# Expert stages that gather and scatter by exact 0/1 matrices over split tokens and rows

## The chip, the core and the metric

The kernel runs on one core of a Trainium2 chip, in one launch. TensorE (PE) multiplies, VectorE (DVE), ScalarE (ACT) and GpSimd (POOL) work beside it, and SyncE (SP) issues nearly all loads of weights from the chip's memory. The metric is the device time of the launch in microseconds (us).

## The reference, cut to what matters

Two transformer blocks of two layers each run over 256 tokens of 1024 features, all in float32. The change is in the second block, whose layers end in a mixture of experts: each token picks two of 32 experts, and each expert is a gated product of width 512.

```python
experts = grp[:, None] * EXPERTS_PER_GROUP + top_local        # two per token
gates = p_grp * jax.nn.softmax(top_logit, axis=-1)
...
def expert_block(args):
    xb, e = args
    return (jax.nn.silu(xb @ w_gate[e]) * (xb @ w_up[e])) @ w_down[e]
...
y_assign = y_slots[dest] * g_sorted[:, None].astype(h.dtype)
y = jax.ops.segment_sum(y_assign, tok_sorted, num_segments=t)
...
x = x + hybrid_mixer(rmsnorm(x, norm_mix[l]), ...)
x = x + hierarchical_moe(rmsnorm(x, norm_ffn[l]), ...)
```

All 32 experts' three matrices are read in each layer: 32 x 6 MiB.

## The kernel before

The tokens lie in two tiles of 128 (t = 0, 1). Each expert has 64 slots; a token sits in the slot that its place among the expert's tokens gives (`pos`, from 1 on; 0 for a token that is not the expert's). Four experts' slots, 256, are one group, and two experts are a pair `pr`.

For a group, `normed` builds `one`, a matrix from tokens to slots: the row of a token holds, in its slot, the token's norm factor `rt.r`. It is made by `hots`, one DVE step for each expert and token tile (L1667). `weighted` builds `wt` in the same way with the expert's gate as the factor. `gather` multiplies the token tiles, as they stand in `h` (float32, the features of a chunk eight apart), by `one` (L1684): 8 chunks of features by 2 token tiles, 256 columns each. ACT and DVE copy the sums, times the norm's gain, into `xg` (L1697, L1695). It also transposes `wt` on PE (L1701), and ACT copies the result to `back` (L1703).

For each expert `gate_up` multiplies its 64 slots by the gate and up weights (L1714), and ACT and DVE form silu(gate) x up (L1718, L1719). `turn` transposes that (L1725, L1727). For each pair `down` multiplies by the down weights (L1737), and ACT and DVE copy the two sums to `ys` (L1742, L1743). `scatter` multiplies `ys` by `back` into `total` (L1749), four banks that hold the sums for all tokens until the layer's end. A pair's scatter stands on PE behind the next pair's first `gate_up`.

PE gives a float32 product two passes in the trace (two rows each). Products of tiles of type fp32r take one pass; elsewhere in the kernel, as in `mm3` (L332 to L334), operands are split into an fp32r high part and an fp32r rest, and three such products stand for one exact product.

The order of each engine's work is the order in which the code issues it. Weights come through a ring of tiles of 1 MiB in the order of use: `Ring.pump` issues a load on SP's queue (L143) as soon as a tile of the ring is free, and a tile becomes free when its last product is done. The ring has 5 tiles for the whole kernel, 8 for the second block, 2 from each layer's output projection on, and `RING3` more in the expert stage. SP's queue works in order. At pair 1 stands `leftover`: SP and the other engines read the largest number of tokens of an expert and branch (L1613, L1614); the branch is not taken here. Loads that are issued behind it in the code wait for it.

## Time and profile before

| | us |
|---|---|
| median of 3 runs | 2049.39 |
| lowest and highest run | 2048.31, 2050.05 |
| span of the profiled execution | 2045.9 |
| PE busy | 1912.5 (93%) |
| PE's weight loads busy | 1452.7 (71%) |
| DVE busy | 800.5 (39%) |
| ACT busy | 653.5 (32%) |

Only the span of the profiled execution is known; the runs' times, which include what lies around a span, are 2.4 to 4.2 us above it. A busy engine is not a bound by itself: PE's passes overlap, and the stages differ in what they wait for. So the page is read by stretches: which engine has no gaps there, and what the others, and the queue of loads, wait for. A window's row gives the stretch and its length in us, then the busy us (and the number of instructions) of PE, PE's weight loads, DVE, ACT and POOL, and last the clock that TensorE was granted (1.00 is 2.4 GHz, 0.50 is 1.2 GHz), the DMA engines' share and GB/s; a window asked for SP has only the last three. Row after row of a timeline or chain begins with start and length in us.

### The profile page before, as it was taken

To read this page: it belongs to the slowest core of one execution; us is meant where nothing else is said; L and a number is where in the kernel's file an instruction comes from. 1 tells how busy PE (TensorE), PEld (TensorE's weight loads), DVE (VectorE), ACT (ScalarE), POOL (GpSimd) and SP (SyncE) were. 2 spreads that over 40 slices of the span, in tenths; PEclk is the share of its full clock that TensorE was granted. 3 is DMA by queue.
4 is the path that set the end of the run, shared out by engine and by line. 5 is a ranking of instruction groups with operands and counts; after the bars stand their busy time and mean duration, and the time that the engine had idled before them with its cause. 6 is when DMAs were issued, how large, how long until landed. Compare 5 with 4: busy or idle time off the path is not lost. (4 is left out here: it accounts for less than half of the span.)

```text
span 2045.9 us, 29429 instructions
## 1 busy us (share of the span) xinstructions
PE 1912.5 (93%) x11967; PEld 1452.7 (71%) x11967; DVE 800.5 (39%) x1946; ACT 653.5 (32%) x1395; POOL 135.5 (7%) x126
## 2 busy tenths in 40 slices
PE   8489999998889999999899999998999999999997
PEld 6367999876679997876566666665776666666664
DVE  6264655566875556772111111012772111111011
ACT  6154544555664446551111101112551111101111
POOL 0042000033320002000000000001000000000000
PEclk9788999999999999999999999999999999999999
DMA  9742656453227554658899999998359999999991
GB/s 245 170 144 73 231 190 211 130 163 122 76 87 243 186 200 130 262 190 355 360 411 413 416 412 414 412 412 295 124 185 367 367 411 413 416 412 413 412 412 45
DMA packets 170172, 559.14 MB, mean 273 GB/s; under 512 B 10176, under 2 KB 69992, under 8 KB 137200
## 3 DMA queue, kind: packets, MB, share of 16 engines
q1 hardware_dynamic: 167056, 546.47, 69.7%
q0 software_dynamic: 2976, 10.74, 3.1%
q8 instruction: 96, 1.57, 0.3%
q14 instruction: 44, 0.36, 0.1%
HBM read 551.40 MB, written 5.77 MB: 272 GB/s over the span
## 5 line engine op out<-in xcount | busy, mean ns | idle before, releaser
L1714 PE MATMUL wps<-wring,X 128*64 128x256 f32 x4096 | 474.9, 380 | 0.0
L1714 PEld LDWEIGHTS wps<-wring,X 128*64 128x64 f32 x4096 | 339.0, 137 | 121.1 <-issue 9.7
L204 DVE TENSOR_TENSOR wlo<-wring,whi 128x1024 fp32r<-128x1024 f32 (+1 forms) x247 | 257.4, 1084 | 100.4 <-ACT whi L196 100.0
L196 ACT CAST whi<-wring 128x1024 fp32r<-128x1024 f32 (+1 forms) x283 | 254.8, 944 | 61.3 <-DMA wring<-in_w_in_ab_dram 39.8
L1737 PE MATMUL wps<-wring,aT 128*64 128x512 f32 x1024 | 248.3, 595 | 0.0
L332 PE MATMUL wps<-xh,whi 128*128 128x256 f32 x832 | 235.9, 284 | 2.6 <-ACT xh L376 2.6
L333 PE MATMUL wps<-xl,whi 128*128 128x256 f32 x832 | 233.8, 281 | 1.4 <-DVE xl L389 1.4
L334 PE MATMUL wps<-xh,wlo 128*128 128x256 f32 x832 | 233.5, 281 | 0.0
L1719 DVE TENSOR_TENSOR a<-a,wps 128x256 f32<-128x256 f32 x64 | 26.9, 421 | 501.0 <-ACT a L1718 501.0
L1737 PEld LDWEIGHTS wps<-wring,aT 128*64 128x64 f32 x1024 | 115.1, 137 | 105.2 <-issue 57.0
L1718 ACT ACTIVATE a<-wps 128x256 f32<-128x256 f32 x64 | 24.5, 383 | 441.0 <-PE wps L1714 441.0
L332 PEld LDWEIGHTS wps<-xh,whi 128*128 128x128 f32 x832 | 157.6, 189 | 8.6 <-issue 3.3
L333 PEld LDWEIGHTS wps<-xl,whi 128*128 128x128 f32 x832 | 157.2, 189 | 3.3 <-DVE xl L389 1.9
L334 PEld LDWEIGHTS wps<-xh,wlo 128*128 128x128 f32 x832 | 157.8, 190 | 0.0
L332 PE MATMUL acc<-whi,xh 128*128 128x512 f32 (+1 forms) x360 | 149.4, 415 | 8.6 <-ACT whi L196 8.5
L334 PE MATMUL acc<-whi,xl 128*128 128x512 f32 (+1 forms) x360 | 144.3, 401 | 8.1 <-DVE xl L389 7.9
L333 PE MATMUL acc<-wlo,xh 128*128 128x512 f32 (+1 forms) x360 | 144.2, 400 | 2.5 <-DVE wlo L204 2.5
L1684 PE MATMUL wps<-one,h 128*128 128x256 f32 x448 | 114.8, 415 | 6.8 <-DVE one L1667 5.2
L1743 DVE COPY ys<-wps 128x512 f32<-128x512 f32 x32 | 22.1, 691 | 252.4 <-PE wps L1737 252.4
L1684 PEld LDWEIGHTS wps<-one,h 128*128 128x128 f32 x448 | 109.3, 336 | 12.9 <-issue 11.8
L1749 PE MATMUL acc<-ys,back 128*128 128x512 f32 x256 | 118.4, 605 | 0.0
L347 POOL TENSOR_SCALAR ss<-ss 128x1 f32<-128x1 f32 x22 | 5.2, 238 | 1502.5 <-ACT junk L345 1502.3
(358 smaller groups left out, 2367.0 us busy)
## 6 DMA issues: line engine op xcount, KB each, us to landing
wring<-in_w_expert_gate_dram SPq DMA_DIRECT2D x128, 1024.0 KB, 9.6
wring<-in_w_expert_up_dram SPq DMA_DIRECT2D x128, 1024.0 KB, 11.1
wring<-in_w_expert_down_dram SPq DMA_DIRECT2D x128, 1024.0 KB, 13.1
wring<-in_w_ffn_gate_dram SPq DMA_DIRECT2D x22, 1024.0 KB, 9.2
wring<-in_w_ffn_up_dram SPq DMA_DIRECT2D x22, 1024.0 KB, 5.4
wring<-in_w_ffn_down_dram SPq DMA_DIRECT2D x22, 1024.0 KB, 7.0
wring<-in_w_in_dram SPq DMA_DIRECT2D x18, 1024.0 KB, 5.5
wring<-in_w_in_ab_dram SPq DMA_DIRECT2D x10, 1024.0 KB, 11.4
```

The source lines that it names most:

```text
L196: self.nc.scalar.copy(vh, src)
L204: eng.tensor_sub(vl, src, vh)
L332: nc.tensor.matmul(o, lh, rh, start=start, stop=False)
L333: nc.tensor.matmul(o, lh, rl, start=False, stop=False)
L334: nc.tensor.matmul(o, ll, rh, start=False, stop=stop)
L1684: nc.tensor.matmul(o[:, 256 * (k % 2):256 * (k % 2) + 256], tokens[:, t, k, :], one[:, t], start=t + k % 2 == 0, stop=t + k % 2 == 2, skip ...
L1714: nc.tensor.matmul(o[64 * half:64 * half + 64, lo:lo + 256], xg[:, k, 64 * (e % 4):64 * (e % 4) + 64], w[:, c, 256 * half:256 * half + 256 ...
L1718: nc.scalar.activation(a, o[:, 0:256], AF.Silu)
L1719: nc.vector.tensor_mul(a, a, o[:, 256:512])
L1737: nc.tensor.matmul(y[d2][64 * ab:64 * ab + 64, :], aTs[ab][:, j, 64 * hf:64 * hf + 64], ws[ab][:, j, 512 * d2:512 * d2 + 512], start=hf + ...
L1743: nc.vector.tensor_copy(ys[:, 512:], y[1])
L1749: nc.tensor.matmul(total[t][d2], back[:, pr % 2, 128 * t:128 * t + 128], ys[:, 512 * d2:512 * d2 + 512], start=pr == 0, stop=pr == 15)
```

## The change

`one` becomes a matrix of ones and zeros in fp32r, made for four experts in one DVE step for each token tile. The norm factor moves out of it: `split_tokens` multiplies each token tile by it and splits the result into `nh` and `nl`, in the order of the features that the gather wants. The gather runs over both parts, 32 fp32r products. `back` too becomes 0/1 in fp32r, by a comparison; the gates come out of the transposed `wt` as a factor per slot (`gs`, a DVE maximum), and `down` applies them while it splits its sums into two parts, which `scatter` multiplies in turn, 8 fp32r products. `RING3` goes from 5 tiles to 3.

```diff
-    RING2, RING3, SPLIT2, SPLIT3, RINGX = 8, 5, 4, 4, 2
+    RING2, RING3, SPLIT2, SPLIT3, RINGX = 8, 3, 4, 4, 2
...
-            def hots(q, by, out, ts=(0, 1)):
-                """Each slot's token by a factor, for four experts."""
+            def normed(q, ts=(0, 1), out=None):
+
+                out = out or ptile([128, 2, 256], F32R, "one", bufs=1)
                 for t in ts:
+                    nc.vector.tensor_tensor(out[:, t].rearrange("p (e n) -> p e n", e=4), C["iota"].unsqueeze(1).to_broadcast([128, 4, 64]),
+                                            bc(pos[:, t, 4 * q:4 * q + 4], 64), ALU.is_equal)
+                return out
+
+            def weighted(q):
+
+                out = ptile([128, 2, 256], F32, "wt", bufs=1)
+                for t in range(2):
                     for e in range(4):
-                        nc.vector.tensor_scalar(out[:, t, 64 * e:64 * e + 64], C["iota"], pos[:, t, 4 * q + e:4 * q + e + 1], by(t, 4 * q + e),
-                                                ALU.is_equal, ALU.mult)
+                        nc.vector.tensor_scalar(out[:, t, 64 * e:64 * e + 64], C["iota"], pos[:, t, 4 * q + e:4 * q + e + 1],
+                                                gate[:, t, 4 * q + e:4 * q + e + 1], ALU.is_equal, ALU.mult)
                 return out
 
-            def normed(q, ts=(0, 1), out=None):
-                return hots(q, lambda t, e: rt.r[:, t:t + 1], out or ptile([128, 2, 256], F32, "one", bufs=1), ts)
-
-            def weighted(q):
-                return hots(q, lambda t, e: gate[:, t, e:e + 1], ptile([128, 2, 256], F32, "wt", bufs=1))
...
+            nh, nl = (ptile([128, 2, 8, 128], F32R, "n" + n, bufs=1) for n in "hl")
             tokens = h.rearrange("p t (q k) -> p t k q", k=8)
 
+            def split_tokens(t):
+                r = rt.r[:, t:t + 1]
+                nc.scalar.activation(nh[:, t], tokens[:, t], AF.Copy, scale=r)
+                nc.vector.scalar_tensor_tensor(nl[:, t], tokens[:, t], r, nh[:, t], ALU.mult, ALU.subtract)
...
-                        nc.tensor.matmul(o[:, 256 * (k % 2):256 * (k % 2) + 256], tokens[:, t, k, :], one[:, t],
-                                         start=t + k % 2 == 0, stop=t + k % 2 == 2, skip_group_check=True)
+                        for n, part in enumerate((nh, nl)):
+                            nc.tensor.matmul(o[:, 256 * (k % 2):256 * (k % 2) + 256], part[:, t, k, :], one[:, t],
+                                             start=t + k % 2 + n == 0, stop=t + k % 2 + n == 3, skip_group_check=True)
...
-                back = ptile([128, 2, S], F32, "back")
-                nc.scalar.copy(back, pt.rearrange("p (a n) -> p a n", a=2))
-                return xg, back
+
+                pt = pt.rearrange("p (a n) -> p a n", a=2)
+                gs = small.tile([128, 4], F32, name="gs", tag="nm")[:, 0:2]
+                nc.vector.tensor_reduce(out=gs, in_=pt, axis=AX.X, op=ALU.max)
+                back = ptile([128, 2, S], F32R, "back")
+                nc.vector.tensor_scalar(back, pt, 0.0, None, ALU.is_gt)
+                return xg, (back, gs)
...
-                ys = tmp.tile([128, D], F32, name="ys", tag="xn")
-                nc.scalar.copy(ys[:, :512], y[0])
-                nc.vector.tensor_copy(ys[:, 512:], y[1])
+                ys = [tmp.tile([128, D], F32R, name="y" + n, tag="xn") for n in "hl"]
+                g = gs[:, pr % 2:pr % 2 + 1]
+                for d2 in range(2):
+                    s_ = slice(512 * d2, 512 * d2 + 512)
+                    nc.scalar.activation(ys[0][:, s_], y[d2], AF.Copy, scale=g)
+                    nc.vector.scalar_tensor_tensor(ys[1][:, s_], y[d2], g, ys[0][:, s_], ALU.mult, ALU.subtract)
                 return ys
...
-                for t in range(2):
-                    for d2 in range(2):
-                        nc.tensor.matmul(total[t][d2], back[:, pr % 2, 128 * t:128 * t + 128], ys[:, 512 * d2:512 * d2 + 512], start=pr == 0, stop=pr == 15)
+                for n, part in enumerate(ys):
+                    for t in range(2):
+                        for d2 in range(2):
+                            nc.tensor.matmul(total[t][d2], back[:, pr % 2, 128 * t:128 * t + 128], part[:, 512 * d2:512 * d2 + 512],
+                                             start=pr + n == 0, stop=pr + n == 16)
...
             rt.place(0)
+            split_tokens(0)
             one = normed(0, (0,))
...
             rt.tile(1)
+            split_tokens(1)
             rt.place(1)
             normed(0, (1,), one)
```

On PE, a period of the expert stage before, from a pair's first gate product over the scatter of the pair before it to the next gather; in an `order` row, the operation, its tiles and the number in a row:

```order
L1714 MATMUL wps<-wring,X 64x256 x32
L1749 MATMUL acc<-ys,back 128x512 x4
L1725 MATMUL wps<-idg,a 128x128 x2
L1714 MATMUL wps<-wring,X 64x256 x32
L1684 MATMUL wps<-one,h 128x256 x16
L1701 MATMUL wps<-idg,wt 128x128 x4
```

The same place after the change, down to the first two of the gather's products, which alternate between the parts 16 times:

```order
L1728 MATMUL wps<-wring,X 64x256 x32
L1768 MATMUL acc<-yh,back 128x512 x4
L1768 MATMUL acc<-yl,back 128x512 x4
L1739 MATMUL wps<-idg,a 128x128 x2
L1728 MATMUL wps<-wring,X 64x256 x32
L1694 MATMUL wps<-one,nh 128x256
L1694 MATMUL wps<-one,nl 128x256
```

The places on PE are the same; the four products of a scatter are eight, first the high part's into all four banks, and the 16 of a gather are 32.

On DVE, where a layer's routing begins (`pos` is the first tile's slot positions, L317 the first step of the second tile's norm factor, on which its routing rests):

```order
 L1529 TENSOR_SCALAR X<-wps,sm_7627 128x128 x2
 L1600 SCALAR_TENSOR_TENSOR pos<-wps,mem 128x32
-L1667 TENSOR_SCALAR one<-cst_7626,pos,rr 128x64 x4
+L1687 SCALAR_TENSOR_TENSOR nl<-h,rr,nh 128x1024
+L1667 TENSOR_TENSOR one<-cst_7626,pos 128x256
 L317 TENSOR_SCALAR rs_v<-ss 128x1
```

The split of 1024 columns now stands ahead of the slot matrix and of the second tile's routing.

On SP, the loads of weight tiles around the branch:

```order
 L143 DMA wring<-in_w_expert_down_dram 128x2x1024 x4
 L143 DMA wring<-in_w_expert_gate_dram 128x2048 x2
-L143 DMA wring<-in_w_expert_up_dram 128x2048 x2
 L1613 TENSOR_LOAD most
 L1613 ISA x2
 L1614 COMPARE_AND_BRANCH
```

Two loads, of an expert's up weights, move from ahead of the branch to behind it.

## Rows read from the trace of the kernel before

**Rows 1.** The page's slices, 40 of equal length: PE's busy tenths, and GB/s.

```profile
PE   8489999998889999999899999998999999999997
...
GB/s 245 170 144 73 231 190 211 130 163 122 76 87 243 186 200 130 262 190 355 360 411 413 416 412 414 412 412 295 124 185 367 367 411 413 416 412 413 412 412 45
```

**Rows 2.** Window of one period of layer 1's expert stage.

```profile
1656.90:1717.90 61.00, 60.06 (x382) 40.25 (x380) 8.39 (x26) 6.36 (x15) 0.00 (x0) 1.00 1.01 413
```

**Rows 3.** Chain of waits over a period: start, us, engine, tile, line, number of passes.

```profile
1656.98 7.98 PE wps L1684 x32
...
1692.62 7.17 PE wps L1737 x31
...
1707.12 3.63 PE acc L1749 x8
...
1718.03 7.97 PE wps L1684 x32
```

**Rows 4.** Waits of SP's queue, whole span: us in total, times, longest us.

```profile
SPq L143 <- PE wps L1714: 468.4, 243, 16.9
```

**Rows 5.** Windows of DMA: stretch, length, PEclk, DMA share, GB/s.

```profile
1616.00:1668.00 52.00, 1.00 1.02 417
...
1731.00:1732.00 1.00, 1.00 0.88 238
1734.00:1735.00 1.00, 1.00 1.05 442
```

**Rows 6.** Timeline of PE in the first block: products of split operands, start and us.

```profile
640.20 0.28 PE L332 MATMUL wps<-xh,whi 128*128 128x256 f32 x1
...
640.90 0.40 PE L332 MATMUL acc<-whi,ah 128*128 128x512 f32 x1
...
642.98 0.39 PE L332 MATMUL acc<-whi,ah 128*128 128x512 f32 x1
```

**Rows 7.** Groups of instructions, shapes apart: count | busy us, mean ns | idle before.

```profile
L204 DVE TENSOR_TENSOR wlo<-wring,whi 128x1024 fp32r<-128x1024 f32 x183 | 214.8, 1220 | 80.4 <-ACT whi L196 80.1
...
L1484 DVE SCALAR_TENSOR_TENSOR h<-acc,rs,h 128x512 f32<-128x512 f32 x16 | 11.8, 748 | 4.0 <-PE acc L334 3.7
...
L1742 ACT COPY ys<-wps 128x512 f32<-128x512 f32 x32 | 18.7, 586 | 202.1 <-PE wps L1737 195.7 <-issue 6.4
```

**Rows 8.** At layer 1's branch: chain, timeline of DVE, windows as in rows 5.

```profile
1594.37 9.54 PE wps L1684 x32
...
1593.24 1.87 DVE L1667 TENSOR_SCALAR one<-cst,pos,rr 128x64 f32<-128x64 f32 x8 [1.03 <-PEq L1614]
...
1596.00:1598.00 2.00, 0.50 1.01 410
1602.00:1604.00 2.00, 1.00 0.73 303
1602.00:1612.00 10.00, 1.00 0.46 161
```

**Rows 9.** Layer 1's expert stage: first gate products, SP's issues, last bytes (window).

```profile
1548.93 7.13 PE L1714 MATMUL wps<-wring,X 128*64 128x256 f32 x64
...
1550.92 5.55 SPq L143 DMA_DIRECT2D wring<-in_w_expert_down_dram  x4
...
1589.55 2.05 SPq L143 DMA_DIRECT2D wring<-in_w_expert_up_dram  x2
...
1996.00:1998.00 2.00, 1.00 0.26 102
```

**Rows 10.** Layer 0's first and last products; layer 1's last scatter and last addition.

```profile
936.09 0.44 PE L1714 MATMUL wps<-wring,X 128*64 128x256 f32 x2
...
1420.09 3.70 PE L1749 MATMUL acc<-ys,back 128*128 128x512 f32 x8
...
2032.22 3.65 PE acc L1749 x8
...
2035.89 0.69 DVE L393 TENSOR_TENSOR h<-h,acc 128x512 f32<-128x512 f32 x1 [0.17 <-PE acc L1749]
```

More of the change, by code (lines that the diff above doesn't have):

```diff
@@ L1728, in turn, with down @@
                 return aT
-            def down(pr, aTs):
+            def down(pr, aTs, gs):
                 y = [wps(), wps()]
@@ L1783, in moe @@
                 t1 = turn(a1)
-                ys = down(pr, (t0, t1))
-                last = (pr, ys, back)
+                ys = down(pr, (t0, t1), back[1])
+                last = (pr, ys, back[0])
                 xg, back = nxt
```

## Prediction

> **What bounds the kernel now.** I read the slices of the span first [rows 1]. The core's DMA engines move 411 to 416 GB/s in two long plateaus, slices 21 to 27 and 33 to 39, and nowhere else so much; these are the expert stages of the two layers. TensorE has its nines nearly everywhere, so the slices alone do not say which of the two sets the pace there. Next a window of one period, the work of four experts, 61.0 us long [rows 2]: PE is busy 60.06 us of it, DVE 8.39, ACT 6.36, and the DMA share is 1.01. The chain of waits [rows 3] settles it: from one gather to the next (1656.98 to 1718.03, 61.05 us) it runs over PE's gathers, scatters and products and has no step on a weight's arrival. SP's queue, in contrast, waits for PE to give weight tiles free, 468.4 us behind the gate and up products alone [rows 4]. So PE is the pace, and the DMA is just behind it: with a backlog the engines move 417 GB/s, and once in a period, when the queue has run dry, they fall to 238 in a 1 us window [rows 5]. A period loads 24 tiles of 1 MiB. At 417 GB/s a tile takes 2.515 us and a period 60.35 us, against PE's 61.05. This near tie is the core of the prediction.
>
> **What PE loses.** Before, a gather is 7.98 us (16 products, shown as 32 passes) and a scatter 3.63 us (4 products, 8 passes) [rows 3]. The products on split fp32r operands elsewhere in this trace start 0.117 us apart at 256 columns (six between 640.20 and 640.90) and 0.231 us at 512 (nine between 640.90 and 642.98) [rows 6]. So the new gather is 32 x 0.118 = 3.78 us (4.20 less; 0.118 to be on the safe side), the new scatter 8 x 0.23 = 1.84 us (1.79 less). A period has one gather and two scatters: 7.8 us less, PE at 53.3 us. In a layer after its first gate product, 7 gathers and 16 scatters: 29.4 + 28.6 = 58.0 us.
>
> **What ACT and DVE get.** None of it lies on PE's path in a period. The pair of sums that leaves the down product is now two ACT steps (0.59 us each as the copy L1742) and two DVE steps that need the same operands; the nearest DVE row is the 0.75 us of L1484, of the same form and width, and 0.69 (an addition [rows 10]) and 1.22 us (the subtraction of twice the width) bound it [rows 7]. ACT, DVE, DVE in a row is some 2.1 us against 0.7, hidden behind the next expert's 7.13 us of gate and up products [rows 9]. The scatter matrix costs DVE a reduction and a comparison, at most 0.7 us each, behind the 7.2 us down product; ACT's copy goes. Four slot matrices at once are 2 DVE steps in place of 8 taking 1.87 us [rows 8]. DVE goes from 8.4 to some 11 us of a period: no bound.
>
> At a layer's start the token split is on the path: ACT's 128 x 1024 part (some 1.1 us, twice the 0.59 of half the width), then DVE's (1.22 as the subtraction of that size [rows 7], 1.5 as two of L1484; I take 1.3) stands ahead of the slot matrix and of the second tile's routing chain; 0.75 us net. The second split waits for ACT behind the routing's exponentials, and the slot positions queue behind it. In return the two first half gathers shrink from 4.2 to 1.9 us. By these steps (durations of the trace, laid end to end) the first gate product comes 0.9 us earlier in layer 0 (its first gather was slower before than layer 1's) and 1.5 us later in layer 1; between -2 and +3 us each.
>
> **What the DMA then allows.** Take layer 1, times from its first gate product at 1548.93 [rows 9]. The ring is full then. 20 issues stand from 1550.92 to 1589.55 [rows 9]; the engines ran dry at 1603.45 (303 of 417 GB/s in the window from 1602) [rows 8]. 20 x 2.515 = 50.3 us back gives an effective start at 1553.15, that is +4.2. Then SP stands at the branch for the leftover tokens, the slot matrices and a 9.54 us gather follow, and only the next down product releases a tile. From 1602 to 1612 the mean is 161 GB/s: (417 - 161) / 417 x 10 = 6.1 us of transfer are lost [rows 8]. The change brings that release forward: one scatter before it (1.8), the slot matrices (some 0.4), the gather (3.8 at full clock, 5.2 if the clock falls to 0.50 as it did here [rows 8]: 4.3 to 5.7). 6.5 to 7.9 us cover the hole. In the order on SP two tiles now stand behind the branch, but the number issued from the first gate product to the branch stays 20, so the backlog that has to cover the hole is the same. From there PE releases 24 tiles in 53.3 us and the engines need 60.35: they never run dry again. With 18 tiles at hand, 174 are left: +4.2 + 174 x 2.515 = +441.8, with 0.3 for a rest of the hole +442. Before, the last byte came at +447.6 (1996.5, 102 GB/s in the window from 1996) [rows 9].
>
> PE alone would be done at 486.9 - 58.0 = +428.9 (before, the last scatter ends at 2032.22 + 3.65 [rows 10], +486.9). So PE eats up the stock of landed tiles and waits for weights in the last quarter of the layer; the DMA sets the end. After the last byte come 0.5 us of landing, half of the 7.17 us down product (3.6) [rows 3], and the scatter behind the two-part eviction (3.0): +449.4. **Layer 1 gains 37.5 us.** The tail behind it loses 1.4: the new scatter finishes no bank before its fifth of eight products, so the four additions (0.69 each) end 2.1 us after it, not 0.7 [rows 10].
>
> Layer 0 has the same shape: first gate product 936.09, last scatter 1420.09 + 3.70 [rows 10], 487.7 us, so 38.2 less 1.6. Its successor's projection weights queue directly behind the last expert, 2.5 to 3 us a tile, and are needed one after the other behind the scatter, 7 us after the last expert's byte: the first two have landed by then, no wait.
>
> The two tiles fewer cost 2 x 2.515 us a layer, inside the sum. They cost nothing while PE is the pace.
>
> **The sum.** 37.5 - 1.4 + 38.2 - 1.6 - 0.6 (the two starts) = 72.1 us. The profiled span of 2045.9 becomes 1973.8; the runs' median lies 3.5 above the span, so **1977 us**. Unknowns: the rate under backlog (414 to 419 GB/s: +6.4 to -4.2 over both layers), the hole (0 to 3 us each), the starts, and up to 4 us a layer where PE, waiting for weights, meets the end at a lower clock.
>
> One rule speaks against the rate on which this stands. The Trainium skill (DMA: Bandwidth & Descriptors, Where 436 GB/s comes from) has loads from HBM held near 358 GB/s, and 435 as the fabric's ceiling. The trace disagrees with the first by its 417. By the second, an estimate of 2.41 us a tile from that page, the sum would be that of rival 1.
>
> **Rivals.** (1) The DMA has more in it than 417: single 1 us windows show 442 [rows 5]. Tiles of 2.4 us or less leave PE as the pace: 486.9 - 57.4 = +429.5, both layers some 112 us less after the tails: 1937. Against it, the 417 holds over a backlogged stretch of 52 us [rows 5]. 5%.
>
> (2) PE's idle moments pull its clock down. After its idle moment at the branch the granted clock stood at 0.50, 1.2 GHz [rows 8]. A PE that waits for weights will idle about 2.3 us before a pair's down product (its two tiles take 5.03 us to come, of which the last gate product, the turn and their evictions fill 2.7). As long as PE still keeps up, the loss is absorbed; it decides when the mean clock over the expert stages falls below 53.3 / 61.05 = 0.87. At 0.8 a period is 66.6 us: 16 x 5.6 = 90 us slower, 2139. Against it: waits start only when the stock is gone, late in a layer, and the 0.94 us of gaps in a period left the clock at 1.00 [rows 2]. 4%.
>
> (3) The 0/1 products gain nothing: weight loading, not the format, sets their pitch. Then a gather stays 32 x 0.249, PE stays at 61 us, the smaller ring costs nothing, and the starts and tails add 3.6: 2053. Against it, the pitch in rows 6 holds with a new stationary operand for each product. 3%.
>
> **How the numbers follow.** Forecast 88%. Its own range is 1966 to 1996 by the unknowns above: -4 -4 below, +6 +6 +5 above, rounded. I keep that as the range; what lies outside is rivals 1 to 3 (12%) and a little of the forecast. About 0.2% (4 us) is what a measurement tells from no change. Faster: forecast and rival 1, 0.93; same: rival 3, 0.03; slower: rival 2, 0.04.
>
> **What would show it.** Right: expert plateaus at 416 to 417 GB/s with no dip at the branch, lasting to within some 8 us of the last scatter; PE waiting for the DMA of weight tiles only in the last two periods of a layer; gathers of 3.8 and scatters of 1.84 us; early periods of 53 us, late ones of 60. Wrong: periods of 53 us to the end (rival 1), a clock under 0.9 in the plateaus (rival 2), an unchanged 7.98 us gather (rival 3), or early dips of the DMA, which would mean that fewer tiles in the ring starve it.

## The result: 2000.5 us, faster by 49 us where 72 were forecast

The changed kernel takes **2000.51 us** (median, 1998.88 to 2001.00) against 2049.24 for the kernel before; the ratio is 0.976 with a 95% interval of 0.9746 to 0.9774. The direction was right, the time lies 4.5 us above the top of the range. The profiled execution spans 1998.4 us (before: 2045.9), so the two traces can be laid beside each other stretch by stretch. In every run that lists both, the time is 1.6 to 2.1 us above the span; the traced execution of the kernel before was thus some 1.5 us faster than its median, and the spans differ by 47.5 us where the medians differ by 48.7.

The slices of the page after (PE's busy tenths, GB/s), which answer to [rows 1]:

```profile
PE   8489999999889999997899999997897999998996
...
GB/s 248 164 151 83 232 190 191 168 131 146 71 64 232 190 193 166 175 273 166 379 417 417 416 416 417 416 417 402 315 169 203 388 416 416 417 416 417 417 416 272
```

The plateaus rose from 411 to 416 to 416 to 417, and PE has lost nines in layer 1's end. The chain of waits over the first group of layer 1 that is comparable with [rows 3] (start, us, engine, tile, line, passes), then two windows of a period each (as in [rows 2]), then SP's waits over the span (as in [rows 4]):

```profile
1628.81 4.03 PE wps L1694 x32
...
1673.23 2.07 PE acc L1768 x8
...
1682.58 4.04 PE wps L1694 x32
```

```profile
1682.58:1736.35 53.77, 52.83 (x381) 38.46 (x381) 10.10 (x24) 7.47 (x16) 0.00 (x0) 1.00 1.02 416
...
1790.11:1850.16 60.05, 54.60 (x380) 34.16 (x380) 10.09 (x24) 7.46 (x16) 0.00 (x0) 1.00 1.02 416
```

```profile
SPq L143 <- PE wps L1728: 222.8, 122, 21.7
...
SPq L143 <- DMA wring<-in_w_expert_down_dram: 170.6, 86, 2.4
```

The gather fell from 7.98 to 4.03 us and the scatter from 3.63 to 2.07. The early periods last 53.77 us and are PE's; the period from 1790.11 on is 60 us, with PE idle 5.4 of them, and it is the DMA's. In layer 1 PE waits for a weight tile for the first time at 1808 (timeline of PE):

```profile
1808.22 1.95 PE L1728 MATMUL wps<-wring,X 128*64 128x256 f32 x16 [0.54 <-DMA wring<-in_w_expert_up_dram]
```

SP waited 468.4 us for PE behind the gate and up products, now 222.8; in return it waits for the transfer eight before, 171 us behind the down tiles alone.

Five landmarks of the two traces give the account. The first gate products of after, and the first attention product behind layer 0's experts (line's products: min/median/max ns, first and last start), the latter in both kernels, after and before:

```profile
938.71 1.04 PE L1728 MATMUL wps<-wring,X 128*64 128x256 f32 x6
...
1530.23 1.08 PE L1728 MATMUL wps<-wring,X 128*64 128x256 f32 x8
```

```profile
L1358 PE MATMUL acc<-kT,qT x32: 376/376/480, 1435.3 to 1468.5; 64*128 64x256 f32 x32
```

```profile
L1358 PE MATMUL acc<-kT,qT x32: 376/376/480, 1459.3 to 1492.3; 64*128 64x256 f32 x32
```

The last scatters of after end as these rows of PE say, 1395.53 + 1.10 = 1396.63 in layer 0 and 1985.72 + 1.10 = 1986.82 in layer 1 (in the brackets: idle time before, and what ended it):

```profile
1390.30 3.65 PE L1752 MATMUL wps<-wring,aT 128*64 128x512 f32 x14 [1.40 <-DMA wring<-in_w_expert_down_dram]
...
1395.53 1.10 PE L1768 MATMUL acc<-yl,back 128*128 128x512 f32 x4
```

```profile
1980.49 3.65 PE L1752 MATMUL wps<-wring,aT 128*64 128x512 f32 x14 [1.30 <-DMA wring<-in_w_expert_down_dram]
...
1985.72 1.10 PE L1768 MATMUL acc<-yl,back 128*128 128x512 f32 x4
```

| stretch | before, us | after, us | change | forecast |
|---|---|---|---|---|
| to layer 0's first gate product | 936.1 | 938.7 | +2.6 | -0.9 |
| layer 0: first gate product to last scatter | 487.7 | 457.9 | -29.8 | -38.2 |
| last scatter to first attention product | 35.5 | 38.7 | +3.2 | +1.6 |
| first attention product to layer 1's first gate product | 89.7 | 94.9 | +5.2 | +1.5 |
| layer 1: first gate product to last scatter | 486.9 | 456.6 | -30.3 | -37.5 |
| last scatter to the end | 10.0 | 11.5 | +1.5 | +1.4 |
| sum | | | -47.6 | -72.1 |

Of the 24.5 us that are missing, the two expert stages hold 15.6, the two starts 7.2, the stretch between the layers 1.6. The first row also holds what moved ahead of the second block: from layer 0's first attention product (844.03 before, 843.30 after) to its first gate product the start takes 92.06 and 95.41 us, +3.4, so the two starts lost 8.0 us against the forecast.

### The profile page after: what moved, and what is told of

It reads as the page before. It is cut to its first block, busy times and chain, and to the rows that moved or that the text cites. A ratio compares the mean times of both kernels' runs of the same rounds, so it can differ in the third digit from the quotient of the medians.

```text
span 1998.4 us, 29447 instructions
## 1 busy us (share of the span) xinstructions
PE 1816.1 (91%) x11967; PEld 1399.4 (70%) x11967; DVE 835.6 (42%) x1918; ACT 679.5 (34%) x1415; POOL 135.8 (7%) x126
## 5 line engine op out<-in xcount | busy, mean ns | idle before, releaser
L1728 PE MATMUL wps<-wring,X 128*64 128x256 f32 x4096 | 480.6, 381 | 15.5 <-DMA wring<-in_w_expert_up_dram 15.3
L1761 DVE SCALAR_TENSOR_TENSOR yl<-wps,gs,yh 128x512 fp32r<-128x512 f32 x64 | 48.0, 751 | 254.3 <-ACT yh L1760 252.7
L1760 ACT ACTIVATE yh<-wps,gs 128x512 fp32r<-128x512 f32 x64 | 43.9, 688 | 230.2 <-PE wps L1752 220.1
L204 POOL TENSOR_TENSOR wlo<-wring,whi 128x1024 fp32r<-128x1024 f32 (+1 forms) x36 | 88.1, 2461 | 134.5 <-ACT whi L196 78.8
L334 PEld LDWEIGHTS acc<-whi,xl 128*128 128x128 f32 x360 | 71.0, 197 | 27.4 <-DVE xl L389 9.7
## 6 DMA issues: line engine op xcount, KB each, us to landing
wring<-in_w_in_ab_dram SPq DMA_DIRECT2D x10, 1024.0 KB, 11.5
```

The costliest lines, as they stand in the source:

```text
L204: eng.tensor_sub(vl, src, vh)
L334: nc.tensor.matmul(o, ll, rh, start=False, stop=stop)
L1728: nc.tensor.matmul(o[64 * half:64 * half + 64, lo:lo + 256], xg[:, k, 64 * (e % 4):64 * (e % 4) + 64], w[:, c, 256 * half:256 * half + 256 ...
L1760: nc.scalar.activation(ys[0][:, s_], y[d2], AF.Copy, scale=g)
L1761: nc.vector.scalar_tensor_tensor(ys[1][:, s_], y[d2], g, ys[0][:, s_], ALU.mult, ALU.subtract)
```

## The experiments

Unless a kernel is said to start from the kernel before, its edit is against the changed kernel. "Stage" is the stretch from a layer's first gate product to its last scatter, layer 0's then layer 1's.

| run | median us | ratio to before (95%) | stages, us |
|---|---|---|---|
| changed kernel | 2000.5 | 0.976 (0.9746, 0.9774) | 457.9, 456.6 |
| gather_only | 2003.2 | 0.9787 (0.9771, 0.9803) | 463.2, 458.1 |
| scatter_only | 1999.9 | 0.9771 (0.9755, 0.9787) | 461.8, 460.0 |
| light_gather | 1999.6 | 0.977 (0.9753, 0.9786) | 458.6, 457.9 |
| ring_less | 2005.9 | 0.9794 (0.9778, 0.9811) | 460.7, 459.9 |
| before_ring3 | 2047.5 | 0.9999 (0.999, 1.0008) | 487.6, 485.7 |
| split_behind | 1990.9 | 0.9719 (0.9706, 0.9732) | 458.0, 457.6 |
| contig_split | 1997.0 | 0.9758 (0.9743, 0.9772) | 461.1, 458.5 |
| reorder_only | 2037.0 | 0.9958 (0.9941, 0.9974) | 481.7, 479.7 |
| no_branch | 1992.3 | 0.9733 (0.972, 0.9746) | 453.8, 453.3 |
| pool_body | 1995.4 | 0.9745 (0.9731, 0.9758) | 458.2, 453.5 |
| late_branch | 2022.9 | 0.9878 (0.9863, 0.9893) | 483.9, 452.8 |
| mid_branch | 1999.9 | 0.9766 (0.9753, 0.9779) | 458.1, 457.3 |
| mid_pool | 1993.0 | 0.9734 (0.9721, 0.9748) | 454.5, 452.9 |
| bank_order | 1999.1 | 0.9763 (0.9749, 0.9776) | 458.1, 457.3 |
| best2 | 1987.5 | 0.9707 (0.9694, 0.972) | 458.6, 453.5 |
| best3 | 1984.9 | 0.9694 (0.9681, 0.9707) | 454.2, 453.2 |

An interval is some 5 us wide, and the kernel before itself read between 2046.1 and 2049.2 us beside these runs, so differences of 3 us are read from the traces' stretches, not from the medians. A landmark in a trace itself moves by 1 to 2 us from one kernel to another where nothing was edited (layer 0's first gate product stands at 936.1 in the kernel before and at 934.2 in before_ring3; the stretch between the layers lasts 37.6 to 38.9 us in the kernels that scatter as the changed one does).

### Does the DMA set the end?

**gather_only** and **scatter_only** each do one half of the change.

```diff
 gather_only (f32 scatter of the kernel before)
-                ys = [tmp.tile([128, D], F32R, name="y" + n, tag="xn") for n in "hl"]
+                ys = tmp.tile([128, D], F32, name="ys", tag="xn")
 scatter_only (f32 gather of the kernel before, no token split, five ring tiles)
-                        for n, part in enumerate((nh, nl)):
-                            nc.tensor.matmul(..., part[:, t, k, :], one[:, t], ...)
+                        nc.tensor.matmul(..., tokens[:, t, k, :], one[:, t], ...)
```

> Only the gather is changed, the scatter is as before. Theory 1 (the DMA sets the end of a layer's experts, whatever TensorE could do below it): TensorE loses 7 x 3.95 us a layer (gather 7.98 to 4.03), so it would end 486.9 - 27.7 = 459.2 us after the first gate product, some 3 us behind the 455.9 to 457.9 of the changed kernel; the tails are a little shorter: 2002 to 2008 us, nearly the whole gain. Theory 2 (the gains of the two parts add up; the measured gain is small because each part is worth about half of what was forecast): some 31 us of the 61 won in the two expert stages remain, the losses at the starts stay: 2025 to 2032 us.

> Only the scatter is changed; no token split, no loss at the layer starts, five ring tiles as before. Theory 1 (DMA cap): TensorE loses 16 x 1.57 us a layer (scatter 3.63 to 2.07) and ends at 486.9 - 25.1 = 461.8 us after the first gate product, above the DMA's 450 to 452 with its two more tiles; so 2 x 25 us less 3 to 4 us in the tails: 2002 to 2006 us, as fast as with both parts. Theory 2 (gains add up, each about half of what the pitch tells): 2020 to 2025 us.

Measured: 2003.2 and 1999.9 us. Each half alone brings nearly the whole gain, and the scatter alone all of it: its stages are 3 to 4 us longer than the changed kernel's, and from the first attention product to the first gate product it is 3.6 us shorter in either layer, because no token split stands there. Theory 2 (additive gains) falls by 20 us and more. With one half alone PE is still the pace: behind the branch every period of a layer lasts 57.7 us (scatter alone) or 57.1 (gather alone), and PE has hardly a wait for an expert's weights in either. One half takes PE down to about the DMA's cap; with both, PE meets it. The stages hit what was worked out from PE's rows, 461.8 and 460.0 us for the scatter alone where 461.8 was expected.

**light_gather** takes 14 us of PE's work out of a layer, **ring_less** one ring tile, **before_ring3** two ring tiles of the kernel before.

```diff
 light_gather
-                        for n, part in enumerate((nh, nl)):
+                        for n, part in enumerate((nh,)):
 ring_less
-    RING2, RING3, SPLIT2, SPLIT3, RINGX = 8, 3, 4, 4, 2
+    RING2, RING3, SPLIT2, SPLIT3, RINGX = 8, 2, 4, 4, 2
 before_ring3, from the kernel before
-    RING2, RING3, SPLIT2, SPLIT3, RINGX = 8, 5, 4, 4, 2
+    RING2, RING3, SPLIT2, SPLIT3, RINGX = 8, 3, 4, 4, 2
```

> The changed kernel with the gather's products on the tokens' low parts left out (half of the gather's products, so this part of the result is missing; the split is still made). TensorE has some 2 us less per group of four experts, 14 us a layer. Theory 1 (DMA cap): only what lies ahead of the DMA counts, the gather halves at the layer start (1.7 us each on the path) and the gather at the branch (2 us earlier release): 4 to 8 us faster than the changed kernel, 1993 to 1997 us. Theory 2 (TensorE still sets the pace, with something else in its way): 28 us and more, 1972 us or less.

> The changed kernel with one ring tile less in the expert stages (2 in place of 3). Theory 1 (DMA sets the end): one tile more has to come after the first gate product, 2.515 us a layer, 5 us in all, and no more: 2005 to 2007 us. Theory 2 (the wait for free ring tiles, not the bytes, sets the end): either nothing, 2000 to 2001 us, if the ring is deep enough, or the DMA falls below its plateau all through a layer and the loss is over 15 us.

> The kernel before with three ring tiles in the expert stages in place of five, nothing else. Theory 1 (before, TensorE is the pace by a near tie: two tiles more to come after the first gate product are 5.0 us of transfer, against 39 us by which TensorE ends behind the last byte): 0 to +2 us, 2048 to 2051 us. Theory 2 (before, the DMA is already the bound somewhere in each layer, so a smaller ring costs at once): +5 to +10 us, 2053 to 2058 us.

Measured: 1999.6 us without half the gather's products, with stages not a microsecond shorter (458.6 and 457.9): 28 us of PE's work are worth nothing, so the end is the DMA's. One ring tile less costs 5.4 us and lengthens the stages by 2.8 and 3.3 us, about a tile's 2.5 each. In the kernel before, two tiles less cost nothing (ratio 0.9999). So the core of the prediction, a cap at some 2.515 us a tile behind PE's old pace, is shown. light_gather also missed its own expectation of 4 to 8 us: an earlier release at the branch was expected to shorten the hole in the DMA there, and it did not. That led to the third question below.

### What did the starts lose?

In layer 1 of after, ACT's and DVE's split steps, and PE's first products of either half gather (timelines; in brackets the idle time before):

```profile
1511.94 2.13 ACT L1686 ACTIVATE nh<-h,rr 128x1024 fp32r<-128x1024 f32 x1
...
1514.11 2.05 DVE L1687 SCALAR_TENSOR_TENSOR nl<-h,rr,nh 128x1024 fp32r<-128x1024 f32 x1 [0.70 <-ACT nh L1686]
...
1523.44 2.05 DVE L1687 SCALAR_TENSOR_TENSOR nl<-h,rr,nh 128x1024 fp32r<-128x1024 f32 x1 [2.51 <-ACT nh L1686]
```

```profile
1516.64 0.55 PE L1694 MATMUL acc<-one,nh 128*128 128x256 f32 x1 [3.46 <-DVE rs_v L317]
...
1526.20 0.55 PE L1694 MATMUL acc<-one,nh 128*128 128x256 f32 x1 [4.71 <-DVE rg L1585]
...
1529.54 0.32 PE L1694 MATMUL acc<-one,nl 128*128 128x256 f32 x1
```

2.13 and 2.05 us where 1.1 and 1.3 stood in the sum; PE stands 3.46 and 4.71 us, the granted clock stands at 0.50 (1.2 GHz) behind the waits, and the halves' products come 0.21 us apart, so that a half takes 3.5 us, not 1.9.

```profile
1520.00:1531.00 11.00, 6.09 (x34) 5.46 (x35) 7.87 (x27) 5.47 (x9) 0.00 (x0) 0.56 0.00 0
```

In that window the mean clock is 0.56; in the same stretch of the kernel before, where PE had stood 1.30 us in front of each half, it was 1.00:

```profile
1538.00:1549.00 11.00, 9.36 (x42) 8.91 (x44) 9.03 (x46) 3.44 (x8) 0.00 (x0) 1.00 0.90 381
```

**split_behind** takes the split off the path. **contig_split** keeps the parts in the order of h: the split then reads without a step, and the gather reads with one.

```diff
 split_behind (the first group's products are those of the kernel before)
-            split_tokens(0)
-            one = normed(0, (0,))
+            one = normed_f(0, (0,))
...
             xg, back = gather(0, one, weighted(0), banks)
+            for t in range(2):
+                split_tokens(t)
 contig_split
-            nh, nl = (ptile([128, 2, 8, 128], F32R, "n" + n, bufs=1) for n in "hl")
+            nh, nl = (ptile([128, 2, 1024], F32R, "n" + n, bufs=1) for n in "hl")
+            kq = lambda n: n.rearrange("p t (q k) -> p t k q", k=8)
...
-                nc.scalar.activation(nh[:, t], tokens[:, t], AF.Copy, scale=r)
+                nc.scalar.activation(nh[:, t], h[:, t], AF.Copy, scale=r)
...
-                            nc.tensor.matmul(..., part[:, t, k, :], one[:, t],
+                            nc.tensor.matmul(..., kq(part)[:, t, k, :], one[:, t],
```

> The changed kernel with the first four experts' gather as before (f32 tokens, the factor in the slot matrix) and the token split behind it, beside the first gate and up products. Theory 1 (the split in front of the first gather is what the starts lost, 3.3 us in layer 0 and 5.1 in layer 1 against the kernel before, and the DMA's stream starts that much later): both come back, 8 us: 1991 to 1994 us, with the first gate product 3.3 us earlier in layer 0 and 8 us earlier on the clock of the trace in layer 1. Theory 2 (the start lost its time by TensorE's lower clock after the wait, which would come whatever the order): at most 3 us, 1997 to 2000 us.

> The changed kernel with the token parts kept in the order of h, so that the split reads and writes them in a row and the gather's stationary operands read them 32 bytes apart. Theory 1 (the stride is what makes the ACT part 2.13 and the DVE part 2.05 us in place of the forecast 1.1 and 1.3): the two fall to about 1.2 and 1.4 us, and each layer's start gains 1.5 to 2.5 us: 1995 to 1998 us. Theory 2 (the size sets the duration, 2 us for 1024 elements of this form): both stay at 2.0 to 2.1 us and the time at 2000 to 2001. A price on the other side: if weight loads with a stride are slow, the gathers grow from 4.03 us.

Measured: split_behind 1990.9 us, 9.6 less. Layer 0's first gate product comes 4.0 us earlier than in the changed kernel, layer 1's stretch from the first attention product to the first gate product is 89.68 us, as in the kernel before (89.67; 91.0 in before_ring3, with the same code there), and the stages are unchanged. From 1490 to 1520, layer 1's start in split_behind, the granted clock is 1.00 throughout. Theory 1 stands: the loss of the starts came from the split's place, the lower clock with it.

contig_split, ACT's and DVE's steps in layer 1:

```profile
1509.72 1.14 ACT L1687 ACTIVATE nh<-h,rr 128x1024 fp32r<-128x1024 f32 x1
...
1511.10 1.28 DVE L1688 SCALAR_TENSOR_TENSOR nl<-h,rr,nh 128x1024 fp32r<-128x1024 f32 x1
```

They fall to 1.14 and 1.28, what the prediction had taken from rows of steps without a stride. So the form was costed rightly and the access pattern not: `tokens` reads h with a step of eight f32. The first gate products come 4.3 us (layer 0) and 2.9 us (layer 1's stretch) earlier. The price came where it had been named: every gather of contig_split takes as long as the f32 gather of [rows 3] had. Its chain, and its weight loads beside those of the changed kernel and of the kernel before (busy us, mean ns of one):

```profile
1626.11 7.92 PE wps L1695 x32
```

```profile
L1695 PEld LDWEIGHTS wps<-one,nh 128*128 128x128 f32 x64 | 21.5, 336 | 1.5 <-issue 1.5
```

```profile
L1694 PEld LDWEIGHTS wps<-one,nh 128*128 128x128 f32 x64 | 12.3, 191 | 1.5 <-issue 1.5
```

```profile
L1684 PEld LDWEIGHTS wps<-one,h 128*128 128x128 f32 x96 | 23.2, 337 | 1.2 <-issue 1.2
```

Split operands in fp32r, read with the old step, gain nothing: a load of 128 x 128 takes 336 ns in place of 191, and the pitch of the products is that of the f32 gather, 0.25 us. That is rival 3's mechanism; the changed kernel escapes it because its split also reorders. **reorder_only** asks whether the order alone would do.

```diff
 reorder_only, from the kernel before
+            nt = ptile([128, 2, 8, 128], F32, "nt", bufs=1)
...
-                        nc.tensor.matmul(..., tokens[:, t, k, :], one[:, t], ...)
+                        nc.tensor.matmul(..., src[:, t, k, :], one[:, t], ...)
...
             xg, back = gather(0, one, weighted(0), banks)
+            for t in range(2):
+                nc.scalar.copy(nt[:, t], tokens[:, t])
```

> The kernel before, in f32 throughout, with one edit: from the second group on the gather reads its stationary operands from a copy of the tokens in the order of use, in place of h with a step of 32 bytes; one ring tile makes room for the copy; the scatter is as before. It tells apart what made the gather fall from 7.98 to 4.03 us. Theory 1 (the step of 32 bytes alone: the gather with parts split exactly but read with that step took 7.96 us): the gather falls to 3.8 to 4.1 us and the time to about that of the kernel with the changed gather alone, 2000 to 2008 us. Theory 2 (order and format are both needed: an f32 pass of 512 columns and 128 stationary columns takes 0.454 us in the scatter, so one of 256 columns takes about half): the gather falls to 6.9 to 7.3 us, 7 x 0.9 us a layer, 2034 to 2042 us.

```profile
1647.74 7.10 PE wps L1686 x32
```

Measured: 7.10 us a gather, its weight loads 190 ns. Order alone gives 0.9 us, format alone none, both together 3.95. Theory 2 stands.

### What makes the hole at the branch?

Layer 1 of after, windows of the DMA and SP's issues:

```profile
1582.00:1584.00 2.00, 2.00 (x12) 1.12 (x10) 0.00 (x0) 0.00 (x0) 0.00 (x0) 1.00 1.00 418
1584.00:1586.00 2.00, 2.00 (x12) 1.17 (x10) 0.00 (x0) 0.00 (x0) 0.00 (x0) 1.00 0.54 221
1586.00:1588.00 2.00, 2.00 (x17) 1.54 (x15) 0.21 (x1) 0.94 (x2) 0.00 (x0) 1.00 0.05 16
1588.00:1590.00 2.00, 2.00 (x22) 2.00 (x20) 1.20 (x2) 0.33 (x1) 0.00 (x0) 1.00 0.97 266
```

```profile
1569.28 2.07 SPq L143 DMA_DIRECT2D wring<-in_w_expert_gate_dram  x2
1587.09 0.81 SPq L143 DMA_DIRECT2D wring<-in_w_expert_up_dram  x2
```

The down product behind the gather, on PE's timeline:

```profile
1579.72 7.18 PE L1752 MATMUL wps<-wring,aT 128*64 128x512 f32 x31
```

(417 - 221 + 417 - 16 + 417 - 266) / 417 x 2 = 3.6 us are lost, where 0.3 was forecast. SP resumes at 1587.09, but PE had been done with the first tiles of the down product since about 1579.72 + 3.66 = 1583.4 (half of it). SP's waits in the window from 1560 to 1592 of after name the place, and the same row for the whole span of the kernel before was there to be read:

```profile
SPq L1614 <- SPq L1614: 14.2, 7, 2.6
```

```profile
SPq L1614 <- SPq L1614: 25.4, 8, 10.6
```

L1614 is the branch. In the order of the changed kernel on SP the instruction that ends it waits for all eight DMA semaphores:

```order
208 L1614 UNCONDITIONAL_BRANCH [waits DMAHW0_49,DMAHW1_49,DMAHW2_49,DMAHW3_49,DMAHW4_49,DMAHW5_49,DMAHW6_49,DMAHW7_49]
```

The traces show when these eight waits were over, first and last, at layer 1's branch of after and then of the kernel before:

```profile
L1614 SPq EVENT_SEMAPHORE  x8: 17/17/17, 1572.8 to 1586.9; - x8
```

```profile
L1614 SPq EVENT_SEMAPHORE  x8: 17/17/17, 1603.5 to 1606.8; - x8
```

If that is it, the hole is a drain: SP issues nothing until every tile in flight has landed, whatever PE releases. In the kernel before, PE's release came last, and so looked like the cause (timelines of SP and PE): SP issued again at 1608.17, when half of the down product from 1604.50 on was done.

```profile
1608.17 1.13 SPq L143 DMA_DIRECT2D wring<-in_w_expert_gate_dram  x2
```

```profile
1604.50 7.45 PE L1737 MATMUL wps<-wring,aT 128*64 128x512 f32 x31
```

But the drain had ended only 1.4 us earlier, so an earlier release could bring SP's next issue forward by no more than that. Four edits and one pair tell the drain from a late PE.

```diff
 no_branch
-                    leftover(l, rt, total)
-                    nc.scalar.preload_act_table_set(SILU)
 pool_body (all four transfers inside the branch)
-                    nc.sync.dma_start(rd[:, t], rest)
+                    nc.gpsimd.dma_start(rd[:, t], rest)
 late_branch
-                    leftover(l, rt, total)
-                    nc.scalar.preload_act_table_set(SILU)
...
                 nxt = gather(pr // 2 + 1, one, wt) if turning else (xg, back)
+                if pr == 15:
+                    leftover(l, rt, total)
 mid_branch (mid_pool: this and pool_body's edit)
-                if turning and pr > 1:
+                if turning and pr != 9:
...
-                if pr == 1:
+                if pr == 9:
                     leftover(l, rt, total)
```

> The changed kernel without the branch for leftover tokens (the path is not taken with these inputs; the count and the branch are left out). Theory 1 (the branch delays TensorE's release of ring tiles, and so makes the hole in the DMA: 3.6 us lost in layer 1, 4.6 in layer 0): the hole closes all but 0 to 2 us, the end comes 5 to 8 us earlier: 1992 to 1996 us. Theory 2 (the hole comes from the stretch without a release itself, gather plus half a down product, while the DMA has too little in stock so early in a layer): the dip stays, 0 to 3 us: 1997 to 2000 us.

> The changed kernel with the transfers inside the branch for leftover tokens issued from GpSimd's queue in place of SyncE's (the path is not taken). In the order on SyncE the branch then ends without a wait for the eight DMA semaphores. Theory 1 (the hole in the DMA at the branch is a drain: SyncE stands at the branch's end until every weight tile in flight has landed, and issues nothing meanwhile): the hole closes as without the branch, 3.5 to 4.5 us in each layer, 1992 to 1995 us. Theory 2 (TensorE's later release behind the branch, 2 us of waiting and a gather at half clock, makes the hole): the dip stays at over 2 us a layer, 1998 to 2001 us.

> The changed kernel with the branch for leftover tokens moved behind the last experts' up product. Theory 1: as without the branch early in the layer (the hole in the DMA closes), and at the layer's end TensorE waits 1 to 2 us for the last weights anyway, which hides part of the branch's 2 to 3 us: 1993 to 1999 us. Theory 2 (the branch costs what it costs, wherever it stands): 2000 to 2002 us.

> The changed kernel with the branch for leftover tokens at the end of the tenth pair of experts in place of the second, its transfers still on SyncE's queue. Theory 1 (the hole is a drain of the weight tiles in flight, wherever the branch stands): a hole of 3.5 to 4.5 us stays in both layers, only later in each: 1998 to 2001 us. Theory 2 (the hole is made by TensorE's late release, early in a layer, when the DMA has little in stock): both holes close, 1992 to 1995 us.

> The changed kernel with both: the branch at the end of the tenth pair of experts, and its transfers on GpSimd's queue. If the hole has two causes that overlap (the drain on SyncE, and in layer 0 TensorE's late release, 3 us of idle time on issue and a gather at half clock) and both act in layer 0: both layers' holes close, TensorE's lost time at the branch is absorbed in the stock of landed tiles, as without the branch: 1991 to 1994 us. If in layer 0 something else holds SyncE: 1995 to 1996 us, as with the transfers moved alone.

Measured: without the branch 1992.3 us; both holes close and the stages are 4.1 and 3.3 us shorter. The same 12 us of layer 1 in no_branch:

```profile
1578.00:1590.00 12.00, 12.00 (x90) 9.45 (x88) 1.92 (x3) 2.13 (x4) 0.00 (x0) 1.00 1.02 421
```

pool_body, whose branch ends on SP without that wait, closes layer 1's hole (453.5 us) and not layer 0's (458.2). There SP now waits for PE (window from 975 to 1003 of pool_body), and PE's timeline of after shows why it is late behind layer 0's branch (pool_body stands 2.75 us at the same place):

```profile
SPq L143 <- PE wps L1752: 17.5, 2, 15.0
```

```profile
982.40 0.36 PE L1694 MATMUL wps<-one,nh 128*128 128x256 f32 x1 [2.21 <-DVE one L1667]
...
987.39 0.58 PE L1694 MATMUL wps<-one,nl 128*128 128x256 f32 x1 [3.11 <-issue]
...
991.28 0.60 PE L1711 MATMUL wps<-idg,wt 128*128 128x128 f32 x4
```

The gather takes 8.9 us there, with 3.11 us of idle time on issue in it, and the granted clock at 0.50 from 983.5 to 990.3. So in layer 0 two causes overlap, the drain and a late release. mid_branch leaves the drain and moves the branch to where SP is 24 us behind PE (in layer 1 they reach it at 1812 and 1788), so that tiles released by PE are waiting for SP: the holes stay, 1999.9 us, only later in each layer, and in layer 1 SP's next eight issues, from 1829.18 to 1833.07, find their tiles already released. mid_pool takes both away: 1993.0 us, as without the branch. Where SP passes layer 1's branch, windows of mid_branch, then of mid_pool:

```profile
1825.00:1833.00 8.00, 3.09 (x7) 2.31 (x8) 1.74 (x3) 1.54 (x3) 0.00 (x0) 0.50 0.55 195
```

```profile
1820.00:1830.00 10.00, 9.23 (x70) 5.66 (x68) 3.95 (x12) 1.37 (x2) 0.00 (x0) 1.00 1.01 421
```

late_branch went past both expectations, 2022.9 us. Layer 1 gained (452.8), layer 0 lost 26 us: ACT's high part of the last sums waited until SP was past the branch, and SP first issued nine projection tiles and two more, until 1407, and then stood at the branch until all had landed. The same wait stands in mid_branch, where it cost nothing:

```profile
1417.13 1.26 ACT L1760 ACTIVATE yh<-wps,gs 128x512 fp32r<-128x512 f32 x2 [37.76 <-SPq L1614]
```

```profile
1829.91 2.23 PE L1768 MATMUL acc<-yh,back 128*128 128x512 f32 x4 [20.88 <-ACT yh L1760]
```

PE stands 20.9 us in the middle of mid_branch's layer 1, and its stage is no longer than that of the changed kernel (457.3 and 456.6): once more the DMA's cap. That ACT waits because the buffer of its eviction is one that the branch's transfers would fill was read from the code and not tried.

### The tails, and all together

```diff
 bank_order
-                for n, part in enumerate(ys):
-                    for t in range(2):
-                        for d2 in range(2):
+                for d2 in range(2):
+                    for t in range(2):
+                        for n, part in enumerate(ys):
 best2 = split_behind + pool_body + bank_order
 best3 = split_behind + mid_pool + bank_order
```

> The changed kernel with the scatter's eight products in the order of the banks (high and low part of one bank one after the other). Theory 1 (the tails lost 1.5 to 2 us each because no bank is finished before the fifth product): the stretch from the last scatter of layer 0 to the first attention product falls from 38.7 by 1 to 1.5 us, the one from the last scatter of layer 1 to the end from 11.6 by 1 us: 1998 to 1999.5 us, at the edge of what can be told. Theory 2 (the low part's eviction sets when the last scatter can run, so the order gains nothing): 2000 to 2001 us.

> The changed kernel with three edits at once: the first gather in f32 with the token split behind it, the branch's transfers on GpSimd's queue, the scatter in the order of the banks. If the three gains are independent: 2000.5 - 9.5 - 7.5 - 1.5 = 1982 us, 1980 to 1985. If the hole at the branch and the start share a cause, or TensorE becomes what is late once the DMA has no hole: 1986 to 1990 us.

> The changed kernel with the first gather in f32 and the token split behind it, the branch at the tenth pair with its transfers on GpSimd's queue, and the scatter in the order of the banks. If the gains of the start (9.6 us), of the branch (8.2) and of the order (1.4) add up: 1981 us, 1980 to 1984. If TensorE becomes late at the end of a layer once the DMA has neither hole nor late start: 1985 to 1988.

Measured: bank_order 1999.1 us, not to be told from 2000.5; the tail falls from 11.5 to 11.1 us, and is 11.1 in best2 and best3 too, where every kernel with the old order and the new scatter has 11.5 to 11.8. The stretch between the layers falls from 38.7 to 38.3, which lies within the 37.6 to 38.9 of kernels without this edit. The order of the banks is worth 0.5 us at the end, not 1, and nothing that can be told between the layers; where the other 2 us went there is open. best2 missed its sum by 5 us, and layer 0's stage (458.6) shows the hole that pool_body leaves there. best3 is the fastest kernel of the study: **1984.9 us**, ratio 0.9694 (0.9681 to 0.9707), 15.6 us below the changed kernel (13.5 by the two ratios). The gains add up to within 4 us.

## Why the prediction was right and wrong, step by step

- **The near tie and the cap.** Right. PE's periods of 53.77 us (53.3 forecast) give way to 60 us at 416 to 417 GB/s once the stock of landed tiles is gone: PE first waits for a tile at 1808, 278 us into a stage of 457, earlier than "the last quarter". Rival 1 (more than 417) and rival 2 (a falling clock) did not come: the granted clock is 1.00 in the periods in which PE waits 5 us.
- **Gather and scatter.** 4.03 and 2.07 us against 3.78 and 1.84; the cap hides the difference. The reason given was incomplete: the rows of split operands had stationary operands in a row, and the gather's pitch depends on that as much as on the format (contig_split, reorder_only). The order of the split's copy, which the prediction did not weigh, is what let it come true.
- **The hole at the branch: the step that failed.** "Only the next down product releases a tile", so an earlier release would cover it, 0.3 us left. It measured 3.6 us in layer 1 and 4.4 in layer 0 (332, 82, 41 and 295 GB/s in the windows of 2 us from 992 to 1000). SP was not waiting for a release but for its own transfers to land. The 10 us of [rows 8] were two things, a drain that ended at 1606.8 and a release at 1608.17, and only the second could be brought forward. In layer 0 PE's 3.1 us on issue came on top. Without the branch (no_branch) the time is 1992.3 us, within the stated range.
- **The starts: mis-sized.** The split's two steps were costed by rows of unstrided operands, 1.1 and 1.3 us for 2.13 and 2.05. PE then waited 3.46 and 4.71 us in front of the halves, the granted clock stood at 0.50 behind that, and the halves took 3.5 us for 1.9. It is 8.0 us together by the stretches from the first attention products, and it came back with the split moved: split_behind, at 1990.9 us, lies within the range too. Either loss alone would have left the forecast standing; both together put it 4.5 us outside.
- **The last bytes.** In layer 1 the rate falls before the end (303 GB/s from 1976 to 1978, 190 to 1980), and PE has the last tile at +450.3 (1980.49), not +442. The hole explains 3.3 us of it, the falling rate about 2, the plateau's 416.4 in place of 417 about 0.6. Some 2.3 us are bytes that the sum left out and that pass through the same engines: 0.5 MiB of the final norm's weights, which SP issues at 1969.99, and 0.45 MiB on the instruction queues q8 and q14. The start explains next to nothing: the transfer missing in the first 10 us is worth 4.3 us, 4.2 were forecast. From 1980.49 to the end of the last scatter 6.3 us passed; the forecast had 6.6 behind its 0.5 us of landing, for which no run has a row of its own. In layer 0 the last tile comes at +451.6, [1.40 <-DMA] in the row above; projection tiles, issued from 1372.56 on, share the engines with it by then. That sharing as the cause was argued, not tried.
- **Two ring tiles.** Right: 2.5 us each where the DMA is the cap (2.8 and 3.3 for one in ring_less), nothing where PE is (before_ring3).
- **The tails.** +1.5 at the end as forecast; the four additions end 1.8 us behind the last scatter (1986.15 + 2.48) where 2.1 was forecast, though the order of the banks, to which that was put down, is worth only 0.5. Between the layers +3.2 against 1.6.
- **The sum itself.** 442 + 0.5 + 3.6 + 3.0 is 449.1, not 449.4, and the unknowns listed give 1969 to 1994 where 1966 to 1996 was stated; neither changes the outcome.
- **No wait for the projection weights.** Right: between the last scatter and the first attention product no wait of PE names a weight's transfer.

## What to carry to other kernels

Once two resources are within a few per cent of each other, price a saving by what the other one allows: here each half of the change alone was worth nearly all of it. Before a queue's gap is called a wait for a release, read that queue's own waits: a branch whose body issues transfers can drain the queue, and an earlier release does little against that. Cost a new elementwise step, or a new stationary operand, from a row with the same stride, not only with the same shape and form.

## What the hardware showed

- A step of 32 bytes between f32 elements costs ACT 2.13 us in place of 1.14 and DVE 2.05 in place of 1.28 for 128 x 1024, and a weight load of 128 x 128 336 ns in place of 191. The Trainium skill (SBUF — State Buffer, Door 1: The DMA port swizzle) has consecutive reads at full speed only within a line of 16 bytes, four f32, and a price for each new line; the trace agrees in the direction, with these numbers for a step of two lines.
- With a step of 32 bytes a pass of an f32 product and one of an fp32r product of 256 columns take the same 0.25 us; in a row they take 0.22 (7.10 / 32) and 0.126 (4.03 / 32).
- Behind the branch in layer 0 PE stood 3.11 us on issue, 2.75 in pool_body; behind layer 1's it did not. Three packets of the instruction queue q14 lie in that window (from 980 to 990), none in the like window of layer 1. Whether code loading is the cause stays open.
- Before the DMA is on its plateau behind a layer's first gate product, transfer is lost: at 227 and 236 GB/s over the first 10 us of the changed kernel's stages, 4.6 and 4.3 us' worth at 417. It is 4.2 to 4.6 us in all other kernels of the study but light_gather (5.2 and 4.9).
